# A transformer block's MLP on one core: stationary activations interleaved, split weights shifted by column group

## The chip, the cores and the metric

The kernel runs on one core of one Trainium2 chip. The metric is the device time of one execution in microseconds. Three runs of the kernel before took 1486.44, 1486.91 and 1488.79 us; their median, 1486.91 us, is the time before.

## What is computed

One encoder block on a sequence of 256 positions with 2048 channels, in float32. Four mixers side by side (gated linear attention, a Fourier mixer, long convolutions, a short convolution) read one input projection `w_in` and are joined by `w_out`. Then comes cross attention to 256 memory positions (`w_xq`, `w_xkv`, `w_xo`), and then the MLP, in which the change lies:

```
x = x + mix @ w_out
x = x + cross_attention(rms_norm(x, norm_g[1]), mem_n, w_xq, w_xkv, w_xo)
gate, up = split(rms_norm(x, norm_g[2]) @ w_gate_up, 2)      # 2048 -> 2 x 5632
x = x + (silu(gate) * up) @ w_down                           # 5632 -> 2048
return rms_norm(x, final_norm_g)
```

## The kernel before

**High and low parts.** TensorE multiplies in a format with fewer mantissa bits than float32 (`F32R`). So each operand is split: a copy into that format is its high part, and the difference to the original is its low part. A product is the sum of three matmuls: high by high, high by low, low by high.

**Weights.** The host packs all weights in the order of use into slabs of 16 blocks of 128 x 128. `Stream._half` loads a slab by a DMA from SP's queue into `raw` (three buffers) and splits half a slab, 8 blocks or 1024 columns, at a time: ScalarE writes the high part `wh` (L104), VectorE the low part `wl` (L105). A tile of `wh` or `wl` has 1088 columns, 64 more than are used, and the 1024 used ones begin at column `at`. `at` is 48 in those parts of the stream that the table `ROWS` lists, and 8 elsewhere. The last entry of `ROWS`, `(NBLK - 48 * FT, NBLK)`, is the whole MLP: 2112 blocks, of which the last 32 (`HELD`) are split into tiles of their own, without an `at`. `Stream.take` hands out the blocks and keeps two or three halves split ahead of their use.

**Two forms of product.** In `gemm` with `mm` (L318, L319) the weights are stationary, that is, loaded into TensorE's array 128 x 128 at a time, and the activations move through it: 512 columns for the high weights (the 256 high columns and the 256 low ones at once) and 256 columns for the low weights. In `gemm_rows` with `part_rows` (L367 to L369) the activations are stationary and 512 columns of weights move. For each block row k and each half r of the 256 positions there are three matmuls: high activations by `wh`, high activations by `wl`, low activations by `wh`. Each of them loads its stationary tile anew.

**Slots.** An activation block is a slot: a tile of 128 partitions x 512 columns, the high part of 256 positions in columns 0 to 255 and the low part in columns 256 to 511. `split`, `split_scaled` and `split2` write it: ScalarE the high part (L204, L208), VectorE the low part (L196, L200). The small `gap` tiles between pools push what follows to chosen addresses; in the built program every slot of the MLP begins 128 bytes past a multiple of 2048, and the moving rows of the MLP begin a multiple of 64 bytes away from that.

**The MLP.** `gate_up` goes over 11 column groups of 512 columns of gate and of up, each over the 16 slots of `h3` (k from 0 to 15). The first group of gate and the first of up are taken together. Each group's result is turned by VectorE, stored to HBM by POOL's queue as `hidden`, fetched back and split into the 44 slots of `f`. `down` then goes over 4 column groups of 512, each over all 44 slots of `f`. `f` is made of 8 tiles that earlier stages used, 20 new ones, and, last, the 16 tiles of `h3`. The order on each engine is the order in which the program is written; background work (`Background`, polled between matmuls) is woven in by a count of estimated time, which the change doesn't touch.

**A strided load elsewhere.** `Hyena.feed` transposes every second column of a tile (L967, `y[:, t, :]` with the two interleaved), so its stationary operand is read at a step of two elements.

Of the kernel before, what the change touches and what calls it, by code (L numbers as in the profile page):

```python
# [14 lines left out]
F32R = mybir.dt.float32r  # L15
# [7 lines left out]
P = 128  # L23
R = 256
# [5 lines left out]
NBLK = 16 * (40 + 16 + 16 + 32 + 16 + 88) + 16 * FT  # L30
# [8 lines left out]
ROWS = ((0, 512), (704, 768), (880, 944), (NBLK - 48 * FT, NBLK))  # L39
# [20 lines left out]
PI_LO = float(np.nextafter(np.float32(math.pi), np.float32(0)))  # L60


class Stream:


    def __init__(self, tc, pools, W, bg):
        self.tc, self.nc, self.W, self.bg = tc, tc.nc, W, bg
        self.rawp, self.wp = pools
        self.order = []
        self.n = 0  # L70
        self.after = []
        self.halves = []
        self.raw = None
        self.extra = None
        self.places = []

    def _half(self):

        nc, n = self.nc, 8 * len(self.halves)
        if n % 16 == 0:  # L80
            self.raw = self.rawp.tile([P, 2048], F32, name="raw", tag="raw")
            for a, b in zip(CUTS[n], CUTS[n][1:]) if n in CUTS else [(0, 1024), (1024, 2048)] if self.after else [(0, 2048)]:
                (nc.scalar if (n, a) == (0, 0) else nc.sync).dma_start(self.raw[:, a:b], self.W[n // 16][:, a:b])
                if self.after:
                    self.after.pop(0)()
        o = (n % 16) * P
        r = self.raw[:, o:o + 1024]
        if n >= NBLK - HELD:
            parts = []
            for a in (0, 512):  # L90
                wh, wl = self.places.pop(0)
                nc.scalar.copy(wh, r[:, a:a + 512])
                nc.vector.tensor_tensor(out=wl, in0=r[:, a:a + 512], in1=wh.bitcast(F32), op=ALU.subtract)
                parts.append((wh, wl))
            self.bg.dve(1024)
            self.halves.append(parts)
            return
        pool = self.extra if self.extra and len(self.halves) % 4 == 3 else self.wp
        wh, wl = (pool.tile([P, 1088], F32R, name=t, tag=t) for t in ("wh", "wl"))
        at = 48 if any(a <= n < b for a, b in ROWS) else 8  # L100
        wh, wl = wh[:, at:at + 1024], wl[:, at:at + 1024]
        edges = [0, 256, 512, 1024] if n == 0 else [0, 512, 1024] if n == 8 else [0, 1024]
        for a, b in zip(edges, edges[1:]):
            nc.scalar.copy(wh[:, a:b], r[:, a:b])  # L104
            nc.vector.tensor_tensor(out=wl[:, a:b], in0=r[:, a:b], in1=wh[:, a:b].bitcast(F32), op=ALU.subtract)  # L105
        self.bg.dve(1024)
        self.halves.append((wh, wl))
# [60 lines left out]
class Block:  # L168
# [471 lines left out]
    def attention(self):  # L640
        tc, nc, act, st = self.tc, self.nc, self.act, self.st
        with tc.tile_pool(name="atp", bufs=1) as atp, tc.tile_pool(name="kp", bufs=1) as kp, \
                tc.tile_pool(name="qp", bufs=1) as qp, tc.tile_pool(name="vp", bufs=1) as vp, \
                tc.tile_pool(name="mp", bufs=5) as mp:
            self.gap(atp, 192)
            self.gap(qp, 96)
            self.gap(vp, 128)
            oex = [atp.tile([P, 512], F32R, name=f"oex{i}") for i in range(4)]
            pt = [atp.tile([P, 512], F32R, name=f"pt{i}") for i in range(2)]
            qs = atp.tile([P, 32], F32, name="qs")[:, 0:2]  # L650
            o = act[0:8] + oex + act[8:12]
            slot = lambda name, n: dict(kt=kp, q=qp).get(name, vp).tile([P, 512], F32R, name=name, tag=name, bufs=n)
            kv = [([], [], []) for _ in range(4)]

            def ev_q(q, p):
                q.append(slot("q", 8))
                self.split(q[-1], self.merge(p))

            def scales():

                col = self.rstd_begin([[self.acc]], D)
                nc.vector.tensor_scalar(out=qs, in0=col, scalar1=512 ** -0.5, scalar2=None, op0=ALU.mult)
                yield

            heads = []

            def load_kv():

                todo = [(hd, what, i) for hd in range(4) for what in range(2) for i in range(4)]
                parts = []  # L670

                def fetch():
                    if len(parts) < len(todo):
                        hd, what, i = todo[len(parts)]
                        m = mp.tile([P, R], F32, name="mr", tag="mr")
                        o = 4 * hd + i
                        nc.gpsimd.dma_start(m, self.vd[:, o * R:(o + 1) * R] if what else self.kd[o * P:(o + 1) * P, :])
                        parts.append(m)

                for _ in range(5):  # L680
                    fetch()
                yield 4
                for n, (hd, what, i) in enumerate(todo):
                    while hd > len(heads) + 1:
                        yield
                    mark = self.mark()
                    if what == 0:
                        kv[hd][0].append(slot("kt", 8))
                        self.split(kv[hd][0][-1], parts[n])
                    else:  # L690
                        if i % 2 == 0:
                            kv[hd][1].append(slot("vh", 4))
                            kv[hd][2].append(slot("vl", 4))
                        c = slice(i % 2 * R, i % 2 * R + R)
                        self.split2(kv[hd][1][-1][:, c], kv[hd][2][-1][:, c], parts[n])
                    self.keep_place(mark)
                    fetch()
                    yield 1.0

            def scores(hd, q):  # L700
                while len(kv[hd][2]) < 2:
                    yield
                yield
                yield from self.head(q, *kv[hd], pt, o[4 * hd:4 * hd + 4], qs)
                heads.append(hd)

            lp = [list(range(8)), list(range(8, 16))]
            self.bg.add(scales())
            self.bg.add(load_kv())
            gens = []  # L710
            for hd in range(4):
                q = []
                if hd > 1:
                    self.bg.drain(gens[hd - 2], True)
                self.gemm("w_xq", [(4 * hd + i) * P for i in range(4)], self.h2, lambda i, p: ev_q(q, p), first=(4, lp),
                          before=lambda n: n and hd == 0 and self.bg.drain(self.late))
                gens.append(self.bg.add(scores(hd, q)))
            h3 = self.h3 = act[12:24] + act[0:4]

            def ev_o(i, p):  # L720
                self.residual(i, p, V_NG + 32 + i, h3[i] if i < 12 else None)
                if i == 12:
                    st.extra = None

            self.gemm("w_xo", [i * P for i in range(16)], o,
                      ev_o,
                      first=(4, [list(range(12)), list(range(12, 16))]), before=lambda n: n == 1 and self.bg.drain())
            self.late = self.bg.add(self.rest(h3, 12, V_NG + 32))
# [41 lines left out]
    def mlp(self):  # L770
        tc, nc, act = self.tc, self.nc, self.act
        with tc.tile_pool(name="fp", bufs=1) as fp:
            self.gap(fp, 192)
            f = act[4:12] + [fp.tile([P, 512], F32R, name=f"f{i}") for i in range(20)] + self.h3
            with tc.tile_pool(name="gp", bufs=2) as gp:
                self.gate_up(gp, f)
            with tc.tile_pool(name="hp", bufs=1) as hp:
                held = [hp.tile([P, 512], F32R, name=f"held{i}") for i in range(HELD // 2)]
                self.st.places = list(zip(held[0::2], held[1::2]))
                self.down(f)  # L780
# [724 lines left out]
```

## Time and profile before

| | |
|---|---|
| median of three runs | 1486.91 us |
| span of the profiled execution | 1482.6 us |
| TensorE busy | 1468.6 us (99%), 7356 matmuls |
| weight loads busy | 1242.4 us (84%) |
| VectorE busy | 944.4 us (64%) |
| ScalarE busy | 764.0 us (52%) |
| GpSimd busy | 161.6 us (11%) |
| matmuls of L367, L368 and L369 after 750 us | 1056 each |

No execution time is listed for the profiled execution itself; the page gives its span, from its first to its last instruction, and the runs' median stands 4.3 us above it. PE is TensorE's matmul, PEld its load of a stationary tile, DVE is VectorE, ACT ScalarE, POOL GpSimd and SP the queue of most DMAs. A group's row gives the line, the engine, the operation, the tiles written and read, the shapes and the number of instructions; then the busy time in us and the mean duration in ns; then the idle time ahead of them, with what ended it. Rows of windows give the stretch, its length, the busy time and number of instructions of each engine, then the granted TensorE clock, the DMA engines' busy share and GB/s. Rows of the timeline give start and duration in us. Matmuls overlap, so the durations of consecutive ones add up to more than the time they take.

### The profile page before, as it was taken

To read this page: it belongs to the slowest core of one execution; us is meant where nothing else is said; L and a number is where in the kernel's file an instruction comes from. 1 tells how busy PE (TensorE), PEld (TensorE's weight loads), DVE (VectorE), ACT (ScalarE), POOL (GpSimd) and SP (SyncE) were. 2 spreads that over 40 slices of the span, in tenths; PEclk is the share of its full clock that TensorE was granted. 3 is DMA by queue.
4 is the path that set the end of the run, shared out by engine and by line. 5 is a ranking of instruction groups with operands and counts; after the bars stand their busy time and mean duration, and the time that the engine had idled before them with its cause. 6 is when DMAs were issued, how large, how long until landed. Compare 5 with 4: busy or idle time off the path is not lost.

```text
span 1482.6 us, 19388 instructions
## 1 busy us (share of the span) xinstructions
PE 1468.6 (99%) x7356; PEld 1242.4 (84%) x7356; DVE 944.4 (64%) x1378; ACT 764.0 (52%) x1136; POOL 161.6 (11%) x276
## 2 busy tenths in 40 slices
PE   9999999999999999999999999999999999999997
PEld 8778888898898888888888888888888888888886
DVE  6688668778777777877765554555554456444444
ACT  6565655467555656656544444444444445434344
POOL 0220100000000001200042401111110112000000
PEclk9999999999999999999999999999999999999999
DMA  9976554454546555544567766666666666555554
GB/s 359 343 258 213 199 195 162 162 177 166 185 138 215 191 180 201 198 171 154 187 197 245 243 213 216 222 225 227 207 206 215 225 223 224 187 192 195 199 196 145
DMA packets 56718, 306.08 MB, mean 206 GB/s; under 512 B 9486, under 2 KB 11183, under 8 KB 25009
## 3 DMA queue, kind: packets, MB, share of 16 engines
q1 hardware_dynamic: 45920, 281.11, 55.1%
q0 software_dynamic: 10272, 23.09, 5.3%
q8 instruction: 57, 0.93, 0.3%
q10 hardware_dynamic: 432, 0.66, 0.1%
q14 instruction: 37, 0.30, 0.1%
HBM read 291.18 MB, written 13.63 MB: 206 GB/s over the span
## 4 chain that ended last, share of the span: by engine, by line
PE 97%; DVE 1%; ACT 1%; DMA 0%; SPq 0%; issue 0%; DVEq 0%; ACTq 0%
PE pg L368 20%; PE pg L367 20%; PE pg L369 20%; PE pg L318 18%; PE pg L319 10%; PE pm L369 1%; PE pm L368 1%; PE pm L367 1%; PE pm L1006 1%; PE pg L315 1%; PE pg L316 1%; PE pm L763 1%; PE pm L736 0%; DVE wl L105 0%; DMA raw<-in_W 0%; PE pm L1386 0%
## 5 line engine op out<-in xcount | busy, mean ns | idle before, releaser
L105 DVE TENSOR_TENSOR wl<-raw,wh 128x1024 fp32r<-128x1024 f32 (+1 forms) x503 | 611.4, 1217 | 465.1 <-ACT wh L104 459.9
L104 ACT CAST wh<-raw 128x1024 fp32r<-128x1024 f32 (+1 forms) x503 | 523.8, 1043 | 584.5 <-PE pg L369 415.4
L368 PE MATMUL pg<-wl,act 128*128 128x512 f32 (+1 forms) x1170 | 455.6, 389 | 1.5 <-DVE wl L105 1.5
L367 PE MATMUL pg<-wh,act 128*128 128x512 f32 (+1 forms) x1170 | 456.5, 390 | 0.0
L369 PE MATMUL pg<-wh,act 128*128 128x512 f32 (+1 forms) x1170 | 455.4, 389 | 0.0
L318 PE MATMUL pg<-act,wh 128*128 128x512 f32 x1104 | 387.7, 393 | 2.9 <-DVE act L196 2.9
L319 PE MATMUL pg<-act,wl 128*128 128x256 f32 x1216 | 340.7, 280 | 0.0
L368 PEld LDWEIGHTS pg<-wl,act 128*128 128x128 f32 x1170 | 219.9, 188 | 48.2 <-DVE wl L105 3.1
L367 PEld LDWEIGHTS pg<-wh,act 128*128 128x128 f32 x1170 | 219.9, 188 | 47.1 <-issue 1.2
L369 PEld LDWEIGHTS pg<-wh,act 128*128 128x128 f32 x1170 | 219.8, 188 | 45.8
L318 PEld LDWEIGHTS pg<-act,wh 128*128 128x128 f32 x1104 | 207.3, 188 | 48.1 <-DVE act L196 3.3
L319 PEld LDWEIGHTS pg<-act,wl 128*128 128x128 f32 x1216 | 228.5, 188 | 0.8 <-DVE wl L105 0.5
L399 POOL DMA_DIRECT2D hidden<-u x88 | 56.9, 654 | 304.1 <-DVE u L396 302.4
L369 PE MATMUL pg<-wh,f 128*128 128x512 f32 x120 | 46.7, 389 | 0.0
L367 PE MATMUL pg<-wh,f 128*128 128x512 f32 x120 | 46.7, 389 | 0.0
L368 PE MATMUL pg<-wl,f 128*128 128x512 f32 x120 | 46.7, 389 | 0.0
L843 POOL DMA_DIRECT2D xrows<-tmp x48 | 27.7, 584 | 128.8 <-DVE tmp L840 124.2
L196 DVE TENSOR_TENSOR tmp<-pg,tmp 128x256 f32<-128x256 f32 x78 | 32.4, 417 | 4.5 <-ACT tmp L325 3.7
L315 PE MATMUL pg<-act,wh 128*128 128x256 f32 x112 | 31.6, 282 | 0.0
L316 PE MATMUL pg<-act,wh 128*128 128x256 f32 x112 | 31.4, 280 | 0.0
L811 POOL DMA_DIRECT2D tmp<-hidden x44 | 24.3, 559 | 60.8 <-DMA hidden<-u 44.9
L399 POOL DMA_DIRECT2D keys<-k x32 | 20.7, 655 | 81.4 <-DVE k L396 79.2
(293 smaller groups left out, 1201.1 us busy)
## 6 DMA issues: line engine op xcount, KB each, us to landing
raw<-in_W SPq DMA_DIRECT2D x246, 1024.0 KB, 5.0
raw<-in_W SPq DMA_DIRECT2D x11, 512.0 KB, 7.3
hidden<-u POOLq DMA_DIRECT2D x88, 64.0 KB, 3.2
tmp<-hidden POOLq DMA_DIRECT2D x44, 128.0 KB, 3.1
res<-in_xT SPq DMA_DIRECT2D x8, 512.0 KB, 7.6
k<-in_mem SPq DMA_DIRECT2D x8, 256.0 KB, 8.3
k<-in_x SPq DMA_DIRECT2D x8, 256.0 KB, 10.2
keys<-k POOLq DMA_DIRECT2D x32, 64.0 KB, 5.2
```

The costliest lines, as they stand in the source:

```text
L104: nc.scalar.copy(wh[:, a:b], r[:, a:b])
L105: nc.vector.tensor_tensor(out=wl[:, a:b], in0=r[:, a:b], in1=wh[:, a:b].bitcast(F32), op=ALU.subtract)
L196: self.nc.vector.tensor_tensor(out=out, in0=a, in1=b, op=op)
L315: self.nc.tensor.matmul(p[:, 0:R], wh, slot[:, 0:R], start=start, stop=False)
L316: self.nc.tensor.matmul(p[:, 0:R], wh, slot[:, R:512], start=False, stop=False)
L318: self.nc.tensor.matmul(p[:, :], wh, slot[:, :], start=start, stop=False)
L319: self.nc.tensor.matmul(p[:, 0:R], wl, slot[:, 0:R], start=False, stop=stop)
L367: self.nc.tensor.matmul(p, hi, wh, start=start, stop=False)
L368: self.nc.tensor.matmul(p, hi, wl, start=False, stop=False)
L369: self.nc.tensor.matmul(p, lo, wh, start=False, stop=stop)
L399: nc.gpsimd.dma_start(to[:, :, 32 * a:32 * a + 32], u[32 * a:32 * a + 32, :].rearrange("f (b t) -> f b t", t=32))
L843: nc.gpsimd.dma_start(to[:, :, c:c + 32], u[32 * a:32 * a + 32, :].rearrange("t (b f) -> t b f", f=32))
```

## The change

Two things change, both only in the MLP.

*Slots.* Each of the 16 slots of `h3` and the 44 slots of `f` is wrapped in a new class `Laced`. It views the same 512 columns as pairs: the high part of position i lies in column 2i, the low part in column 2i + 1. A slice of 128 high columns, which was 512 contiguous bytes in each partition, becomes 128 elements at a step of 8 bytes, over 1024 bytes. The splits write, and the matmuls' loads read, at that step.

*Weights.* In the MLP `at` is no longer always 48 but 48, 52, 56, 60 in turn, changing every 64 blocks: `wh` and `wl` begin 0, 16, 32 or 48 bytes further on. 64 blocks are 16 steps of k for one column group, that is, 96 matmuls; in `gate_up` a turn is a column group (the first two groups, which are interleaved, share two turns), in `down` a turn ends after 16 of 44 steps. The held last 32 blocks aren't shifted. Of the 3168 matmuls of the MLP 864 keep the distance as it was, and 768 each get 16, 32 and 48 bytes.

```diff
+class Laced:
+    def __init__(self, t):
+        self.t = t.rearrange("p (r two) -> p two r", two=2)
+
+    def __getitem__(self, at):
+        c = at[1]
+        return self.t[at[0], c.start // R, c.start % R:(c.stop - 1) % R + 1]
...
         wh, wl = (pool.tile([P, 1088], F32R, name=t, tag=t) for t in ("wh", "wl"))
-        at = 48 if any(a <= n < b for a, b in ROWS) else 8
+        at = 8
+        for a, b in ROWS:
+            if a <= n < b:
+                at = 48 + (4 * ((n - a) // 64 % 4) if b == NBLK else 0)
...
-            h3 = self.h3 = act[12:24] + act[0:4]
+            h3 = self.h3 = [Laced(t) for t in act[12:24] + act[0:4]]
...
-            f = act[4:12] + [fp.tile([P, 512], F32R, name=f"f{i}") for i in range(20)] + self.h3
+            f = [Laced(t) for t in act[4:12] + [fp.tile([P, 512], F32R, name=f"f{i}") for i in range(20)]] + self.h3
```

## The prediction

> **What bounds the kernel now.** I read the totals and the slices first, then the chain that ended last, then the costliest groups.
>
> ```profile
> span 1482.6 us, 19388 instructions
> PE 1468.6 (99%) x7356; PEld 1242.4 (84%) x7356; DVE 944.4 (64%) x1378; ACT 764.0 (52%) x1136; POOL 161.6 (11%) x276
> PEclk9999999999999999999999999999999999999999
> PE 97%; DVE 1%; ACT 1%; DMA 0%; SPq 0%; issue 0%; DVEq 0%; ACTq 0%
> L105 DVE TENSOR_TENSOR wl<-raw,wh 128x1024 fp32r<-128x1024 f32 (+1 forms) x503 | 611.4, 1217 | 465.1 <-ACT wh L104 459.9
> L104 ACT CAST wh<-raw 128x1024 fp32r<-128x1024 f32 (+1 forms) x503 | 523.8, 1043 | 584.5 <-PE pg L369 415.4
> L368 PE MATMUL pg<-wl,act 128*128 128x512 f32 (+1 forms) x1170 | 455.6, 389 | 1.5 <-DVE wl L105 1.5
> L368 PEld LDWEIGHTS pg<-wl,act 128*128 128x128 f32 x1170 | 219.9, 188 | 48.2 <-DVE wl L105 3.1
> L319 PEld LDWEIGHTS pg<-act,wl 128*128 128x128 f32 x1216 | 228.5, 188 | 0.8 <-DVE wl L105 0.5
> ```
>
> TensorE is the bound: 97% of the chain, the clock granted in full, and before L368 only 1.5 us of idle time in 1170 matmuls. VectorE and ScalarE wait for TensorE, not the other way (ScalarE's cast waits 415.4 us for the last matmul to free its buffer). So only what changes the pace of matmuls can move the time.
>
> The 389 ns of a matmul is not its pace, because matmuls overlap. The pace is the distance between starts. From here on the views are the windows of line L369 and the timeline of TensorE, whose columns are start and duration in us.
>
> ```profile
> 750.00:1482.60 732.60, 410.92 (x1056) 198.21 (x1056) 1.00 0.63 211
> ```
> ```profile
> 760.00:1470.00 710.00, 710.00 (x3137) 587.76 (x3136) 374.08 (x398) 308.11 (x349) 110.57 (x184) 1.00 0.63 212
> ```
> ```profile
> 1000.05 0.39 PE L367 MATMUL pg<-wh,act 128*128 128x512 f32 x1
> ...
> 1009.57 0.39 PE L367 MATMUL pg<-wh,act 128*128 128x512 f32 x1
> ```
> ```profile
> 739.95 0.39 PE L318 MATMUL pg<-act,wh 128*128 128x512 f32 x1
> ...
> 751.04 0.39 PE L318 MATMUL pg<-act,wh 128*128 128x512 f32 x1
> ```
>
> The MLP (from about 754 us on) holds 1056 matmuls of each of L367, L368 and L369: 3168, all of 512 columns. Between the two L367 rows lie 42 steps: 9.52 / 42 = 226.7 ns each. In 760 to 1470 us TensorE is busy in every microsecond, with nothing but these and a few transposes: 710 / 3137 = 226.3 ns. The stage before alternates 512 and 256 columns; between its two L318 rows lie 32 pairs, 11.09 / 32 = 346.6 ns a pair. If a matmul costs c plus a per column, 512a + c = 226.7 and 768a + 2c = 346.6 give 256a = 106.8 and c = 13.1 ns. So 13.1 ns of each matmul go with loading a new stationary tile and not with columns: 3168 x 13.1 = 41.5 us in the MLP, all that a better place in memory could win.
>
> **That this 13.1 ns can grow** is also in the trace. After each piece of background work the same three lines run slower for a while and then fall back:
>
> ```profile
> 159.27 0.39 PE L367 MATMUL pg<-wh,act 128*128 128x512 f32 x1
> ...
> 162.04 0.39 PE L367 MATMUL pg<-wh,act 128*128 128x512 f32 x1
> ...
> 163.40 0.39 PE L367 MATMUL pg<-wh,act 128*128 128x512 f32 x1
> ```
>
> Twelve steps from 159.27 to 162.04 are 230.8 ns each, the next six (to 163.40) 226.7 again, with no wait in between and the same distances of addresses. So there are a settled pace and an unsettled one, 4.1 ns apart. The MLP is settled from end to end. [...]
>
> **The change, part by part.** The two built programs have the same 11887 instructions in the same order with the same buffers, addresses of buffers and waits; only access patterns differ. No DMA, queue or wait moves, so there is nothing new behind any wait.
>
> 1. *Writing the slots interleaved.* 60 slots (16 of h3, 44 of f) are written by a ScalarE cast or scale and a VectorE subtraction, now at a step of two elements. The nearest rows with a strided side are L1406 (writes every second column) and a VectorE product with both sides strided, beside the same operations without:
>
> ```profile
> L1406 ACT COPY res<-pm 128x256 f32<-128x256 f32 x4 | 1.3, 390 | 3.3 <-PE pm L1386 3.3
> L976 ACT COPY x<-pm 128x256 f32<-128x256 f32 x4 | 1.5, 380 | 0.0
> L196 DVE TENSOR_TENSOR res<-pm,x 128x256 f32<-128x256 f32 x4 | 1.7, 421 | 1.1 <-PE pm L1168 1.1
> L196 DVE TENSOR_TENSOR tmp<-pm,tmp 128x256 f32<-128x256 f32 x24 | 9.5, 417 | 3.5 <-ACT tmp L325 3.4
> L204 ACT CAST f<-tmp 128x256 fp32r<-128x256 f32 x20 | 7.9, 402 | 0.0
> L196 DVE TENSOR_TENSOR f<-tmp,f 128x256 fp32r<-128x256 f32 x20 | 8.2, 417 | 0.0
> ```
>
> The last two rows are the splits that change. +10 and +4 ns, times 60: 0.8 us on engines that are busy 308 and 374 of 710 us there. Hidden by the matmuls; 0. Uncovered it would be 0.8 us. Doubled it is still hidden.
>
> 2. *Loading the stationary tile at a step of 8 bytes.* Only one load in the kernel is strided: L967's transposes of every second column. L755's are the same, contiguous.
>
> ```profile
> L967 PEld LDWEIGHTS pm<-ident,tmp 128*128 128x128 f32 x16 | 2.5, 199 | 0.6 <-issue 0.4
> L755 PEld LDWEIGHTS pm<-ident,tmp 128*128 128x128 f32 x16 | 1.9, 140 | 0.9 <-DVE tmp L749 0.6
> ```
> ```profile
> 205.71 0.28 PE L319 MATMUL pg<-act,wl 128*128 128x256 f32 x1
> 205.71 0.32 PEld L967 LDWEIGHTS pm<-ident,tmp 128*128 128x128 f32 x2
> 205.83 0.39 PE L967 MATMUL pm<-ident,tmp 128*128 128x128 f32 x2
> ```
> ```profile
> 312.36 0.28 PE L319 MATMUL pg<-act,wl 128*128 128x256 f32 x1
> 312.36 0.75 PEld L1168 LDWEIGHTS pm<-tab,k 128*128 128x128 f32 x6
> 312.48 0.72 PE L1168 MATMUL pm<-tab,k 128*128 128x128 f32 x5
> ```
>
> A strided load took 199 ns, against 140 for the contiguous transpose and 188 for a plain load. A load begins with the matmul before it and has that matmul's 226.7 ns: with 188 ns some 38 remain, with 199 some 27. It becomes the bound only above about 226 ns. What the matmul under the load suffers is seen once: 0.12 us from L319 to the next start under a strided load, and 0.12 us under a contiguous one (L1168). Price 0 from these rows; ends of the range -13.1 ns (all that goes with the load is gone) and +13.1 ns (what goes with the load doubles, since the load now reaches over twice the bytes). [...]
>
> 3. *The shift of wh and wl.* Until now moving rows and slots lie a multiple of 64 bytes apart in the MLP. In the new program 864 of the 3168 matmuls keep that distance, 768 each get 16, 32 and 48. Distance 32 is seen in the stage before (slots against wh at offset 8), at the same settled cost per load (346.6 ns a pair). Distances 16 and 48 are nowhere in the trace. For these 1536 matmuls I take the unsettled pace, +4.1 ns, because it is the only other pace that these lines show; the ends are -13.1 and +13.1 ns as in 2. ScalarE's and VectorE's writes to the shifted place are contiguous as before: 0.
>
> The sum: 1632 x 0 + 1536 x 4.1 = +6.3 us. On the profiled span 1482.6 -> 1488.9. The median of the runs stands 4.3 us above that span, so 1486.9 + 6.3 = **1493.2 us**, 0.4% slower.
>
> **The rivals.**
>
> *Faster: the two streams stop meeting.* Moving row: 2048 bytes in 226.7 ns. A contiguous stationary tile is 512 bytes and is overtaken; at a step of 8 bytes the load covers 1024 bytes and could run level with the moving row, so that two reads that start apart stay apart. It decides where the distance is right, perhaps at two of the four: 1584 x 13.1 = 20.8 us, 1466. At all four 1445. [...] For: the 13.1 ns goes with loads. Against: 0.12 us under L967, where the load is strided and nothing was won.
>
> *Slower, and more: the load's share doubles.* It covers twice the bytes; +13.1 ns on each matmul, 41.5 us, 1528. The point from which the load alone would bound is 226 ns. Against: again L967's 0.12 us.
>
> *Nothing.* The pace is fixed per load, whatever the addresses: 1486.9. For: the same cost at distances 0 and 32; settled 226.7 ns over the whole MLP although buffers, row halves and high and low parts differ. Against: the unsettled stretch. [...]
>
> **How the numbers follow.** About 0.2% (3 us) is what a measurement can tell from no change. My sum, some distances slower by a few ns: 0.42. Double share or worse: 0.10. Together slower 0.52. Faster rival: 0.36, between 1445 and 1483 by how many distances gain. Nothing: 0.12. The likeliest one's own range is 1490 to 1501 (all 3168 at 4.1 ns). The whole range, with cases of both signs, is 1456 to 1529: it leaves out a gain at nearly all distances (0.09) and more than a doubling (0.05).
>
> **What would show it.** In the new profile the stretches of the MLP differ by shift: a change of pace every 96 matmuls (64 blocks of weights). By my sum the pace is 226.7 ns at shifts 0 and 32 and about 231 at 16 and 48; in the rival some stretches show 213 to 220 ns; with nothing all show 226.7. LDWEIGHTS of L367 to L369 should rise from 188 to about 199 ns. The groups of ScalarE and VectorE splits of f should stay within 10 ns of 402 and 417 ns. The prediction is wrong if a load in the MLP takes over 226 ns, if the pace is the same in all stretches, or if VectorE's wl appears as a releaser of TensorE.

## The result, and the profile after

The kernel after takes 1506.21 us (median of 4 runs, 1506.13 to 1506.42), the kernel before 1486.82 us in the same comparison (4 runs, 1486.44 to 1488.79). The ratio is 1.0131, with a 95% interval of 1.0116 to 1.0145: 19.4 us slower. The forecast was 6.3 us slower.

The profiled execution took 1506.13 us, with this page:

```profile
span 1504.3 us, 19388 instructions
PE 1489.9 (99%) x7356; PEld 1266.6 (84%) x7356; DVE 944.7 (63%) x1378; ACT 765.4 (51%) x1136; POOL 161.6 (11%) x276
PEclk9999999999999999999999999999999999999999
PE 98%; DVE 1%; ACT 1%; DMA 0%; issue 0%; SPq 0%; DVEq 0%; ACTq 0%
L119 DVE TENSOR_TENSOR wl<-raw,wh 128x1024 fp32r<-128x1024 f32 (+1 forms) x503 | 611.5, 1217 | 486.1 <-ACT wh L118 481.3
L382 PE MATMUL pg<-wl,act 128*128 128x512 f32 (+1 forms) x1170 | 460.4, 393 | 1.7 <-DVE wl L119 1.7
L382 PEld LDWEIGHTS pg<-wl,act 128*128 128x128 f32 x1170 | 225.8, 193 | 47.6 <-DVE wl L119 3.1
L333 PEld LDWEIGHTS pg<-act,wl 128*128 128x128 f32 x1216 | 229.3, 189 | 0.8 <-DVE wl L119 0.5
```

Everything but TensorE's pace is as it was: the clock is granted in full, TensorE holds 98% of the chain, and its idle time before L382 (the line that was L368) is 1.7 us against 1.5. VectorE only waits more (486.1 us at L119, against 465.1). TensorE's own busy time went from 1468.6 to 1489.9 us, 21.3 us more, and nearly all of that lies in the MLP (below). The load of L333, which the change doesn't touch, takes 189 ns, against 188.

Windows of TensorE from 810 to 1230 us, inside the MLP, first before, then after (stretch, length, busy time with the number of matmuls, granted clock, DMA share, GB/s):

```profile
810.00:1230.00 420.00, 420.00 (x1855) 1.00 0.66 219
```
```profile
810.00:1230.00 420.00, 420.00 (x1804) 1.00 0.64 215
```

In 420 busy microseconds at full clock there are 51 matmuls fewer: one in 226.4 ns before, one in 232.8 after. From the first to the last start of the MLP's 3168 matmuls the trace has 719.75 us before and 739.69 after: +19.9 us, or 6.3 ns each. That is the result. (The MLP also began 1.8 us later, behind stages that the change doesn't touch.)

By stretch the pace is almost flat. The timeline of the kernel after, two starts 60 matmuls apart, at shifts of 0, 16, 32 and 48 bytes in turn:

```profile
1027.54 0.39 PE L382 MATMUL pg<-wl,act 128*128 128x512 f32 x1
...
1041.54 0.39 PE L382 MATMUL pg<-wl,act 128*128 128x512 f32 x1
...
1049.93 0.39 PE L382 MATMUL pg<-wl,act 128*128 128x512 f32 x1
...
1063.93 0.39 PE L382 MATMUL pg<-wl,act 128*128 128x512 f32 x1
...
1071.86 0.40 PE L383 MATMUL pg<-wh,act 128*128 128x512 f32 x1
...
1085.87 0.40 PE L383 MATMUL pg<-wh,act 128*128 128x512 f32 x1
...
1094.49 0.39 PE L381 MATMUL pg<-wh,act 128*128 128x512 f32 x1
...
1108.43 0.39 PE L381 MATMUL pg<-wh,act 128*128 128x512 f32 x1
```

14.00, 14.00, 14.01 and 13.94 us over 60 steps: 233.3, 233.3, 233.5 and 232.3 ns. Even the stretches with no shift run at 233.3, not 226.7.

Windows of L383 over the MLP (matmuls, then loads) and the two splits of f that write interleaved:

```profile
750.00:1520.00 770.00, 417.32 (x1056) 205.91 (x1056) 1.00 0.59 201
```
```profile
L218 ACT CAST f<-tmp 128x256 fp32r<-128x256 f32 x20 | 8.2, 423 | 0.0
L210 DVE TENSOR_TENSOR f<-tmp,f 128x256 fp32r<-128x256 f32 x20 | 8.2, 419 | 0.0
```

A load takes 205.91 / 1056 = 195.0 ns (before: 198.21 / 1056 = 187.7), far under a matmul's 233. ScalarE's split went from 402 to 423 ns, VectorE's from 417 to 419.

### The profile page after: what moved, and what is told of

Its sections match the earlier page's. It is cut to its first block, busy times and chain, and to the rows that moved or that the text cites. A ratio compares the mean times of both kernels' runs of the same rounds, so it can differ in the third digit from the quotient of the medians.

```text
span 1504.3 us, 19388 instructions
## 1 busy us (share of the span) xinstructions
PE 1489.9 (99%) x7356; PEld 1266.6 (84%) x7356; DVE 944.7 (63%) x1378; ACT 765.4 (51%) x1136; POOL 161.6 (11%) x276
## 4 chain that ended last, share of the span: by engine, by line
PE 98%; DVE 1%; ACT 1%; DMA 0%; issue 0%; SPq 0%; DVEq 0%; ACTq 0%
PE pg L382 20%; PE pg L381 20%; PE pg L383 20%; PE pg L332 18%; PE pg L333 10%; PE pm L381 1%; PE pm L383 1%; PE pm L382 1%; PE pm L1020 1%; PE pg L329 1%; PE pg L330 1%; PE pm L777 1%; PE pm L750 0%; DVE wl L119 0%; PE pm L1400 0%; DMA raw<-in_W 0%
## 5 line engine op out<-in xcount | busy, mean ns | idle before, releaser
L119 DVE TENSOR_TENSOR wl<-raw,wh 128x1024 fp32r<-128x1024 f32 (+1 forms) x503 | 611.5, 1217 | 486.1 <-ACT wh L118 481.3
L382 PE MATMUL pg<-wl,act 128*128 128x512 f32 (+1 forms) x1170 | 460.4, 393 | 1.7 <-DVE wl L119 1.7
L381 PE MATMUL pg<-wh,act 128*128 128x512 f32 (+1 forms) x1170 | 461.3, 395 | 0.3 <-ACT wh L118 0.3
L383 PE MATMUL pg<-wh,act 128*128 128x512 f32 (+1 forms) x1170 | 460.4, 394 | 0.0
L333 PE MATMUL pg<-act,wl 128*128 128x256 f32 x1216 | 341.5, 281 | 0.0
L382 PEld LDWEIGHTS pg<-wl,act 128*128 128x128 f32 x1170 | 225.8, 193 | 47.6 <-DVE wl L119 3.1
L381 PEld LDWEIGHTS pg<-wh,act 128*128 128x128 f32 x1170 | 225.9, 193 | 46.5 <-issue 1.2
L383 PEld LDWEIGHTS pg<-wh,act 128*128 128x128 f32 x1170 | 225.8, 193 | 44.9
L333 PEld LDWEIGHTS pg<-act,wl 128*128 128x128 f32 x1216 | 229.3, 189 | 0.8 <-DVE wl L119 0.5
L383 PE MATMUL pg<-wh,f 128*128 128x512 f32 x120 | 47.4, 395 | 0.0
L382 PE MATMUL pg<-wl,f 128*128 128x512 f32 x120 | 47.4, 395 | 0.0
```

What stands on the lines that cost most here:

```text
L333: self.nc.tensor.matmul(p[:, 0:R], wl, slot[:, 0:R], start=False, stop=stop)
L381: self.nc.tensor.matmul(p, hi, wh, start=start, stop=False)
L382: self.nc.tensor.matmul(p, hi, wl, start=False, stop=False)
L383: self.nc.tensor.matmul(p, lo, wh, start=False, stop=stop)
```

## The experiments

Two theories stood against each other at the outset. *Place*: the pace hangs on where the moving row lies against the stationary tile. *Load*: a strided load costs more by itself, wherever it lies. Unless said otherwise a pace is taken from starts within a stretch of 96 matmuls, and "moved by" is counted from the place that `wh` and `wl` have in the kernel before. There, in the addresses of the built program, every moving row of the MLP begins a multiple of 256 bytes from its stationary tile (the sections ahead of the result speak of multiples of 64, which is true but too loose). Interleaving moves something too: the low part begins 4 bytes behind the high part, no longer 1024, so for a third of the matmuls, low activations by `wh`, the row now begins 4 bytes short of a multiple of 256. In the kernel after only 576 of the 864 matmuls without a shift therefore keep their distance. The experiments are called e1 to e12. The kernel before took 1486.12 us (median of 7) beside e1 to e8, 1486.22 beside e9 to e11 and 1487.01 beside e12.

### One half of the change at a time

Only the interleaved slots (e1; the edit is against the kernel after):

```diff
-        at = 8
-        for a, b in ROWS:
-            if a <= n < b:
-                at = 48 + (4 * ((n - a) // 64 % 4) if b == NBLK else 0)
+        at = 48 if any(a <= n < b for a, b in ROWS) else 8
```

> The interleaved slots alone, with the weights' rows at their old place. Theory A (the strided load costs about 6.3 ns a matmul wherever the rows stand): pace 233 ns throughout the MLP, 1506 us. Theory B (the shift costs, the interleaving is free): 226.7 ns, 1487 us.

Only the shift (e2; the edit is against the kernel before):

```diff
-        at = 48 if any(a <= n < b for a, b in ROWS) else 8
+        at = 8
+        for a, b in ROWS:
+            if a <= n < b:
+                at = 48 + (4 * ((n - a) // 64 % 4) if b == NBLK else 0)
```

> The four shifts alone, with slots stored as before. Theory A: 226.7 ns at all four shifts, 1487 us. Theory B: 226.7 ns at shift 0 and 32, slower stretches at 16 and 48 (231 ns or more), 1493 us or more.

| | time, us | ratio to before | MLP, first to last start | load |
|---|---|---|---|---|
| interleaved only | 1509.18 (4 runs) | 1.0158 (1.0141 to 1.0175) | 742.92 us | 196 ns |
| shift only | 1501.65 (4 runs) | 1.0103 (1.0088 to 1.0118) | 733.73 us | 188 ns |
| both | 1506.21 (4 runs) | 1.0131 (1.0116 to 1.0145) | 739.69 us | 195 ns |

Each half loses alone, 23.1 us and 15.5 us against the 1486.12 beside them, and together they lose less than the first alone: they don't add up. What the shift breaks can be seen by itself, with loads as short as before. Timeline of "shift only" at 0, 16, 32 and 48 bytes, 60 steps each:

```profile
1030.98 0.39 PE L371 MATMUL pg<-wl,act 128*128 128x512 f32 x1
...
1044.58 0.39 PE L371 MATMUL pg<-wl,act 128*128 128x512 f32 x1
...
1052.38 0.40 PE L372 MATMUL pg<-wh,act 128*128 128x512 f32 x1
...
1066.28 0.40 PE L372 MATMUL pg<-wh,act 128*128 128x512 f32 x1
...
1074.43 0.40 PE L371 MATMUL pg<-wl,act 128*128 128x512 f32 x1
...
1088.43 0.40 PE L371 MATMUL pg<-wl,act 128*128 128x512 f32 x1
...
1097.06 0.40 PE L372 MATMUL pg<-wh,act 128*128 128x512 f32 x1
...
1111.06 0.40 PE L372 MATMUL pg<-wh,act 128*128 128x512 f32 x1
```

13.60, 13.90, 14.00 and 14.00 us: 226.7, 231.7, 233.3 and 233.3 ns. So the place matters by itself, with nothing else changed, and the pace comes back in the stretches that aren't moved (227.2 over all of them). Distance 32 was expected at 226.7 and ran at 233.3. In "interleaved only" the weights stay where they were, and the pace is still lost. The 4 bytes by which the low parts move don't explain it as a distance alone: with contiguous slots a row 4 bytes short of a multiple of 256 ran at 228.0 ns (e12, below). Whether the step itself costs, or that two distances now alternate among the matmuls, no run separates. The starts of e1 alternate:

```profile
1040.20 0.39 PE L380 MATMUL pg<-wh,act 128*128 128x512 f32 x1
1040.43 0.40 PE L378 MATMUL pg<-wh,act 128*128 128x512 f32 x1
1040.67 0.39 PE L379 MATMUL pg<-wl,act 128*128 128x512 f32 x1
1040.90 0.40 PE L380 MATMUL pg<-wh,act 128*128 128x512 f32 x1
1041.14 0.39 PE L378 MATMUL pg<-wh,act 128*128 128x512 f32 x1
```

Steps of 0.23, 0.24, 0.23, 0.24 us, in the trace's nanoseconds 229 and 238 in turn for most of a stretch. This isn't a disturbance that dies down. The unsettled pace is a fixed pattern that repeats itself.

The same addresses don't always give the same pattern, though. From the first column group of `down` on e1 runs at 235.6 ns to the end, in steps of 238, 234 and 235 ns. Here are 60 steps of the 25th stretch of 96, first in e1, then in the kernel after, where this stretch has no shift and its 96 matmuls read the same addresses in the same order:

```profile
1297.54 0.40 PE L378 MATMUL pg<-wh,act 128*128 128x512 f32 x1
...
1311.67 0.40 PE L378 MATMUL pg<-wh,act 128*128 128x512 f32 x1
```
```profile
1297.62 0.39 PE L381 MATMUL pg<-wh,act 128*128 128x512 f32 x1
...
1311.62 0.39 PE L381 MATMUL pg<-wh,act 128*128 128x512 f32 x1
```

14.13 and 14.00 us: 235.5 and 233.3 ns. The 11 stretches of `down` at 2.2 ns more make 2.3 us, most of the 3.2 us by which e1's MLP is longer than that of the kernel after; the stretches at shift 48 (232.2 ns instead of 233.3) make most of the rest. The first stretch of e2 at 48 bytes shows the like:

```profile
828.95 0.39 PE L370 MATMUL pg<-wh,act 128*128 128x512 f32 x1
...
842.75 0.39 PE L370 MATMUL pg<-wh,act 128*128 128x512 f32 x1
```

13.80 us, 230.0 ns, against 233.3 in the stretch at 48 bytes shown above, again with the same addresses in the same order. So the addresses don't settle the pattern by themselves. What else does wasn't tested; what ran just before is one candidate.

### Longer steps, and a load that reads one element

Four parts interleaved, so that a tile is read at a step of 16 bytes over 2048 bytes (e3; no shift, but the four kinds of tiles begin 0, 4, 8 and 12 bytes past a slot's start):

```diff
-        self.t = t.rearrange("p (r two) -> p two r", two=2)
+        self.t = t.rearrange("p (i r two) -> p two r i", two=2, r=2)
...
```

> Slots with high and low parts of both halves of the positions interleaved four ways, so that the load reads at a step of 16 bytes over 2048 bytes; no shift. If the load's share grows with the bytes that it covers (512: 13.1 ns, 1024: 19.4 ns): 2048 bytes give about 32 ns, a pace of 246 ns, 1548 us. If any step costs the same: 233 ns, 1506 us. If the load itself gets too long (over 226 ns): the pace is the load's, more than 250 ns.

The kernel before with a stationary tile that reads its first column 128 times in the MLP (e4; every tile begins where it did, but the product is another):

```diff
+        if self.st.n > NBLK - 48 * FT:
+            hi, lo = (x[:, 0:1].to_broadcast([P, P]) for x in (hi, lo))
```

> Each load in the MLP reads one column 128 times (step 0); the MLP's result is then not the reference's, all else is as before. If the 13.1 ns that go with a load are its reads of memory beside the moving row's: pace near 213.6 ns, about 1446 us. If they are a fixed price of changing the stationary tile: 226.7 ns, 1487 us.

Windows of L388 over the MLP of the kernel with 16 bytes, then its TensorE from 810 to 1230 us:

```profile
750.00:1520.00 770.00, 419.78 (x1056) 326.88 (x1056) 1.00 0.59 201
```
```profile
810.00:1230.00 420.00, 420.00 (x1789) 1.00 0.63 213
```

The load took 326.88 / 1056 = 309.5 ns, and yet a matmul started every 420 / 1789 = 234.8 ns (1516.12 us, MLP 746.31). So by the trace's times loads overlap each other too, and a load longer than the matmul's pace didn't become the bound. With 114 ns more of load this kernel is only some 1 to 2 ns a matmul slower than the interleaved one with 196 ns. The pace doesn't follow the load's duration.

The one-element tile did neither of the two things expected of it. It got slower: 1499.69 us, MLP 735.35 us, one matmul in 231.4 ns:

```profile
810.00:1230.00 420.00, 420.00 (x1815) 1.00 0.64 215
```

It reads a 128th of the distinct bytes and is slower than 128 contiguous elements, with loads of 189 ns. So the price doesn't shrink with the distinct bytes of a load (that the load makes 128 reads all the same is possible; the trace doesn't show reads). What falls of *Load* is that the pace follows a load's duration or its span of bytes. That a tile which isn't contiguous costs something by itself stays: in e4 every tile begins where it did, and a matmul loses 5.0 ns.

### Which distances hold the pace

Steps of 64 bytes (e5, moved by -192, -128, -64 and 0) and of 4 bytes (e6, 0, 4, 8 and 12), contiguous slots:

```diff
+                at = 16 * ((n - a) // 64 % 4) if b == NBLK else 48
```

> Slots as before; the weights' rows of successive groups moved by -192, -128, -64 and 0 bytes instead of 0, 16, 32 and 48. If only the place within 64 bytes matters: 226.7 ns in all stretches, 1487 us. If the place within 128 or 256 bytes matters: one or two of the four settled at 226.7 ns, the others at 231 to 234 ns, 1495 to 1500 us.

```diff
+                at = 48 + ((n - a) // 64 % 4 if b == NBLK else 0)
```

> Slots as before; the weights' rows of successive groups moved by 0, 4, 8 and 12 bytes. If it is the 16-byte piece that counts in which a row begins: 226.7 ns in all, 1487 us. If every shift unsettles the pace: 226.7 ns at 0 and 230 to 234 ns at 4, 8 and 12, about 1500 us.

Then 33 places in one run, 8 bytes apart, from -192 to +64, a new one for every 96 matmuls; with contiguous slots (e9), and with interleaved ones (e10):

```diff
+                at = 2 * ((n - a) // 64) if b == NBLK else 48
```

> Slots as before; the weights' rows stand 8 bytes further on in each successive stretch of 96 matmuls, from -192 to +64 bytes, so that one run shows the pace at 33 distances. If the settled pace belongs to one distance in 256 bytes alone: 226.7 ns at 0 only, 229 to 238 ns elsewhere, about 1502 us. If there are more good places (or better ones): several stretches at 226.7 ns or less.

> The same scan with interleaved slots. If interleaving takes the settled pace away wherever the rows stand: no stretch at 227 ns or under, a mean of 232 to 235 ns, about 1506 us. If it only moves the good place: one or more stretches at 227 ns or under.

And the places between, 4 bytes off that grid, contiguous slots (e12):

```diff
+                at = abs(2 * ((n - a) // 64) - 1) if b == NBLK else 48
```

> Slots as before; the scan once more at the distances between: 4 bytes past each multiple of 8, from -188 to +60 bytes. If the place of the kernel before is the only settled one: no stretch at 227 ns or under, a mean near 233 ns, about 1507 us. If there is a better place, a version that beats both kernels follows from it: a stretch under 226.7 ns.

| kernel | time, us | MLP, us | pace by place, ns |
|---|---|---|---|
| steps of 64 bytes | 1496.84 | 731.33 | -192: 229.2; -128: 232.4; -64: 233.3; 0: 227.0 |
| steps of 4 bytes | 1502.41 | 735.71 | 0: 227.0; 4: 237.8; 8: 234.1; 12: 229.0 |
| 33 places, contiguous | 1506.31 | 739.09 | 0 (with the held blocks): 227.6; +64 and -192: 229.2; -152: 230.0; the other 29: 231.1 to 236.6, 11 of them 233.2 to 233.4 |
| 33 places, interleaved | 1508.45 | 740.23 | best 230.0 (-96 and -64); 0: 233.1; worst 236.4 (-40) |
| places between, contiguous | 1505.94 | 741.09 | 28, 60 and 108 bytes past a multiple of 256: 227.4 to 227.7, the best; 20: 239.1; 68, 100, 132 and 196: 239.9 to 240.0, the worst |

Timeline of the scan with contiguous slots, at 0 and at +32, 60 steps each:

```profile
1300.07 0.39 PE L370 MATMUL pg<-wh,act 128*128 128x512 f32 x1
...
1313.67 0.39 PE L370 MATMUL pg<-wh,act 128*128 128x512 f32 x1
...
1388.16 0.39 PE L372 MATMUL pg<-wh,f 128*128 128x512 f32 x1
...
1402.16 0.39 PE L372 MATMUL pg<-wh,f 128*128 128x512 f32 x1
```

226.7 and 233.3. Of the interleaved one at -96, its best:

```profile
1030.09 0.39 PE L382 MATMUL pg<-wl,act 128*128 128x512 f32 x1
...
1043.89 0.39 PE L382 MATMUL pg<-wl,act 128*128 128x512 f32 x1
```

230.0. And of the places between at +28 and at +20:

```profile
1366.10 0.40 PE L371 MATMUL pg<-wl,act 128*128 128x512 f32 x1
...
1380.48 0.40 PE L371 MATMUL pg<-wl,act 128*128 128x512 f32 x1
...
1388.25 0.39 PE L371 MATMUL pg<-wl,f 128*128 128x512 f32 x1
...
1401.88 0.39 PE L371 MATMUL pg<-wl,f 128*128 128x512 f32 x1
```

At +20 (the first pair) 239.7 ns, at +28 (the second) 227.2: eight bytes make 12 ns. On this finer grid the places 12, 28, 44 bytes and so on (12 past a multiple of 16) are the faster ones, 227 to 232, and those 4 past a multiple of 16 the slower, 233 to 240. The two scans hold 64 distances, one for every 4 bytes of 256. Of these only the old one settled at 226.7 ns, and none below it. With interleaved slots none of the 33 places came under 230.0. A scan has one stretch for nearly every place, and e2 has shown 230.0 and 233.3 at the same one, so differences of a few ns between the slower places may not be the place's; the places that e2, e5 and e6 share with the scans agree within 1 ns, that stretch apart.

### Distance, or absolute place, or direction

Every tile of activations and of weights 64 bytes further on, distances kept (e11; kernel before):

```diff
+        self.gap(cp, 64)
```

> The kernel before with everything in the memory of the core 64 bytes further on, so that all distances between slots and weights' rows stay. If the distance sets the pace: 226.7 ns, 1487 us. If the place of the moving rows itself does: as with the rows alone 64 bytes from their place, 229 to 233 ns, 1495 to 1508 us.

It took 1485.72 us, MLP 719.84 us. Its TensorE from 810 to 1230 us:

```profile
810.00:1230.00 420.00, 420.00 (x1854) 1.00 0.66 220
```

One matmul in 226.5 ns, as before. Moving the weights alone by 64 bytes gave 229.2, moving everything by 64 bytes 226.7: here it is the distance that counts and not where the tiles lie.

Weights written in reverse within each 512 columns and read at a step of -1, so that the moving row runs backward past the stationary tile; with contiguous (e7), then with interleaved slots (e8):

```diff
+            back = lambda x: x.rearrange("p (a b) -> p a b", b=512)[:, :, ::-1]
...
+            wh, wl = wh[:, ::-1], wl[:, ::-1]
```

> Slots as before, no shift; the weights' rows of the MLP are written back to front and read by the matmuls from the last column to the first, so that the moving operand runs the other way against the load. If the settled pace hangs on how the two reads run against each other: another pace than 226.7 ns (231 to 235 ns, or, if they now pass each other more rarely, under 226 ns). If it is a fixed price per load: 226.7 ns, 1487 us.

> As the run before it, with interleaved slots, so that the load covers 1024 bytes. If two reads that run level stop meeting (the rival that promised a gain), this or the interleaving alone must show it: 213 to 220 ns, 1450 to 1466 us. If every step of 8 bytes costs about 7 ns: 233 ns, 1508 us.

1505.01 us (MLP 740.33) and 1508.30 us (MLP 740.64), in both one matmul in 233.3 ns. TensorE from 810 to 1230 us of the first and the second:

```profile
810.00:1230.00 420.00, 420.00 (x1802) 1.00 0.64 215
```
```profile
810.00:1230.00 420.00, 420.00 (x1801) 1.00 0.64 215
```

The held last blocks, whose matmuls still read forward, ran at 227.4 in the first. Turning the direction costs the same 6.7 ns as interleaving in `gate_up`, or as a move by 32 or 48 bytes, and turning it on interleaved slots costs nothing more. It was tried at this one place only, where the first element read lies 4 bytes short of a multiple of 256. So the kernel before stands in one good arrangement: a contiguous tile, a row read forward, a distance that is a multiple of 256 bytes. Nothing tried that leaves it settled at 226.7; most of it ran at 229 to 240 ns, and 233.3 is the commonest pace.

No version was faster than the kernel before by more than e11's 0.5 us in a single run, which tells nothing.

## Why the prediction was wrong

**What bounds the kernel: right.** TensorE's pace in the MLP carries all of the result (19.9 us more there, 19.4 between the medians), with no new wait; VectorE's wl releases TensorE for 1.7 us, against 1.5 before. That it came out slower, as forecast, is luck: the forecast's loss came from the shift alone, and the kernel loses as much in stretches without a shift, by the interleaving, which had been priced at 0. The base was a little rough: the profiled executions here end 1.8 us above their spans, so some 2.5 of the 4.3 us that the working added to the span were the difference between one execution and another.

**Step 1, writing interleaved: right in its price, wrong in its size.** The splits took 21 and 2 ns more (within 10 was forecast), 60 x 23 ns = 1.4 us if all slots pay as f's do, and no wait shows it.

**Step 2, the strided load: the step that failed.** Its duration was forecast well (199 ns, measured 195), and its price at 0, from one start-to-start step of 0.12 us under L967 and one under L1168. That pair of rows couldn't show it. A single step after a matmul of another shape says nothing of the pace into which a long row of equal matmuls settles, and 0.12 us to two decimals doesn't resolve 7 ns. Measured alone (e1) it is 742.92 - 719.75 = 23.2 us, 7.3 ns on each of 3168. It lies inside the range that was given for it, -13.1 to +13.1, and the chosen value was at the wrong place. In the kernel after, the stretches without a shift run at 233.3 ns, where the sum had 226.7. The term holds all that interleaving brings, the step and the 4 bytes by which the low parts move; the working counted 864 matmuls that keep their distance, and only 576 do.

**Step 3, the shift: the mechanism right, a distance wrong.** A change of pace every 96 matmuls, with 226.7 at shift 0, is what e2 shows. For 16 and 48 bytes the sum had +4.1 ns, and e2 has +5.0 and +6.7. The failed term is distance 32, held to be free because the stage before runs at 346.6 ns a pair there. In the MLP it costs 6.7 ns. That stage has other shapes and its pairs fix the sum of two costs only, so one cost c for both stages was an assumption. Nor is it the same distance: in the built program rows and tiles there lie 160 bytes past a multiple of 256. That is 32 only if nothing but the place within 64 bytes counts, and e5 shows that more counts (229.2 to 233.3 ns at moves by 64, 128 and 192). In the changed kernel this step has nothing left to act on: with interleaved slots the stretches are at 233.3, 233.3, 233.5 and 232.3. Nearly the same pace in all stretches was one of the signs of being wrong that the working had named. (The upper end of its likeliest case, 1501, is 1499.9 by its own figures.)

**"Wrong if a load takes over 226 ns".** None did in the kernel after, but the bound itself was wrong: with loads of 309.5 ns (e3) the pace was 234.8.

**The rivals.** *Faster* needed stretches at 213 to 220 ns. The scans had 64 distances with contiguous slots and 32 with interleaved ones, and none was under 226.7 ns. That two reads running level stay out of each other's way is not seen in any of them. *The load's share doubles* would have been 239.8 ns everywhere; the kernel after has 233.1 on average over the four shifts, half of that step. Only some places of e12 reach 240.0. *Nothing* is ruled out by e2 (226.7 to 233.3 ns by place alone), and by e12, where the same three lines ran at 239.7 ns at the place 20 bytes on and at 227.2 at 28. The load's duration went with the step: 188 ns at 4 bytes, 195 to 196 at 8, 309.5 at 16. The pace didn't go with it: at a step of 8 bytes (e1, MLP) it has already lost 7.3 of the 8.4 ns that it loses at 16 (e3, (746.31 - 719.75) us / 3168).

**What stays open.** Why the arrangement of the kernel before is the one that settles wasn't shown. The runs say that the pace changes with the distance between row and tile (226.7 to 240.0 ns), with the tile's step (231.4 in e4, where all places stay) and with the row's direction (233.3 in e7), and that it doesn't follow the load's duration (234.8 under loads of 309.5 in e3); that these don't fix it alone is seen where the same addresses ran at 233.3 and 235.5 or at 230.0 and 233.3 ns. A trace shows no reads of memory, so whether and where the two meet isn't seen. No run has interleaved slots with both parts a multiple of 256 bytes from the row, so the cost of the step and that of two distances in turn aren't told apart. Reading a stationary tile backward wasn't tried.

## What to carry to other kernels

In this kernel, where matmuls run back to back with a new stationary tile each, the pace hung by up to 6% (240.0 against 226.7 ns) on the distance between the moving row and the stationary tile, so a change of layout in either operand has to be priced by start-to-start steps in a long row of equal matmuls, not by the load's duration or by one step elsewhere. Such a dependence can be read in one run: move one operand by a few bytes every hundred matmuls and take the pace of each stretch. And the costs of two edits that break the same good arrangement didn't add up: 23.1 and 15.5 us made 19.4. A change of layout can also move more than it names: here interleaving moved the low parts by 4 bytes.

## What the runs showed of the hardware that was not expected

- With contiguous tiles the pace of a 512-column matmul with a load of 128 columns was 226.7 ns at one distance of 64 tried, 227 to 240 at the others, and most often 233.3; moving all tiles together by 64 bytes left it (226.5 ns, 226.4 before, in the same windows).
- The slower paces are repeating patterns, such as 229 and 238 ns in turn, that last for whole stretches. The same addresses in the same order ran in more than one of them: at 233.3 and 235.5 ns, and at 230.0 and 233.3.
- Loads of 309.5 ns ran under matmuls that started every 234.8 ns.
- A stationary tile that reads one column 128 times was 5.0 ns a matmul slower (231.4 against 226.4 in the same windows) than 128 contiguous columns, and a moving row read backward 6.7 ns slower (233.1 against 226.4) than one read forward.
